# A hybrid attention and FFN layer on one core: operands of down in the tiles of gate/up, last norms on VectorE, additions on POOL, scores two units ahead, and inputs interleaved

## The chip, the cores and the metric

The kernel runs on 1 core of one Trainium2 chip. The metric is the device time of one execution in microseconds (us). A core has five engines with instruction queues of their own: PE (TensorE, matmuls), DVE (VectorE), ACT (ScalarE), POOL (GpSimd), and SP (SyncE), which here issues all the transfers. Each queue runs in order. SBUF is the working memory, PSUM takes the results of matmuls.

## The reference, cut to what matters

One decoder layer over 1024 tokens of width 1024, in float32. One input projection feeds two groups of heads: four differential-attention heads (each the difference of two softmaxes) and eight heads with three branches (compressed, selected, window). One output projection follows, then a residual, a layer norm, a SwiGLU network of width 2816, a residual and a second layer norm.

```python
h = x @ w_in[l]
...
blk = kv[:, idx] + pe[None, None, :, None, :]          # compress_kv
return jax.nn.gelu(blk @ w1) @ w2
...
a = p[:, :, 0] - lam * p[:, :, 1]                      # diff_attention, per block of queries
...
mix = jnp.concatenate([o_diff, o_nsa], axis=-1) @ w_out[l]
x = layer_norm(DEEPNORM_ALPHA * x + mix, ln1_g[l], ln1_b[l])
ffn = (jax.nn.silu(x @ w_gate[l]) * (x @ w_up[l])) @ w_down[l]
x = layer_norm(DEEPNORM_ALPHA * x + ffn, ln2_g[l], ln2_b[l])
```

## The kernel before

Every float32 operand of a large matmul is split in a high part (the rounded form that TensorE takes, written by ScalarE) and a low part (the rest, by VectorE or POOL: `split`, L81 and L83), and a product is three matmuls, high by high, high by low and low by high (`mm3`, L116 to L118). The function is written in stages. A scheduler of the framework orders the instructions of each engine by their place in the source, moved by explicit priorities, and by a simulated time at which each is ready. Tiles come from pools: a tag with `bufs=n` has n places, and a new tile waits until the old one in its place is no longer used.

*Start.* Three blocks of w_in (`w3`) and x transposed (`load_x`, half of the tokens at a time) are loaded and split; three products run beside each other. The first block of weights is loaded in two pieces ahead of the first piece of x. The low part of the first block is made on VectorE, of the others on POOL. The results are copied out of PSUM (L243 to L247), and `compress` adds the position terms to them (L197, eight instructions), multiplies (L207) and applies gelu. Between these, the weights of values and gates (`w_vg`, three pieces) are split and projected for eight blocks of rows.

*Attention.* Each phase has units of a front (scores, the fused scale, distance and minimum L308, exponentials) and a back (transposes L330, the split of the transposed tile, products with the values). A unit takes one or two of six t tiles. `LOOK` is 1: a unit's back is written after the front of the next unit. Fillers (projections for later phases, loads of w_out) are spread between the units. The last phases are diff(2) and diff(3), in two halves each.

*Output and x.* `out_start` loads a row block of the mixed heads and splits it, `out_half` multiplies by w_out, `norm1` normalises. For the FFN x is cut in four quadrants, and sums of them (T1 to T4, by `x_sums`) feed a Strassen-like scheme with seven products in place of eight. X 11, 21, T3 and T2 have eight tiles of 8 KB per partition in the pool pb, with four half tiles; 22, T1 and T4 lie in big and w tiles.

*Gate and up.* 11 pairs of blocks; each step multiplies by all seven operands, and VectorE and POOL combine the results. The operands of down for each pair are written to DRAM: `hidden_operands` (a_d, L980 to L988) and `down_weights` (t_d, L968 to L974). The order of the products in a step is 11, 21, T3, T1, 22, T2, T4.

*Down.* The pool pb is closed and the pool pc with nine op tiles opened in its place. Seven products of 11 steps each follow, in the order 1, 2, 6, 5, 3, 7 and 4. A step (`down_operand`) loads a piece of a_d and a piece of t_d (L1042, L1043), splits them, and runs 12 matmuls. The first six steps use op tiles, later ones alternate between big and op. Rows 0 to 3 are normalised after product 3, rows 4 to 7 at the end, where the last product runs row by row; of these, two rows use ScalarE, POOL and VectorE in turn (L617 to L619), and two `vector_only` (L609, L611). The reciprocal root (L129, L130) is always on POOL.

Of the kernel before, what the change touches and what calls it, by code (L numbers as in the profile page):

```python
# [17 lines left out]
P = 128  # L18
# [6 lines left out]
NCMP = 63  # L25
WIN_BLOCKS = 5
AHEAD = 1.25
LOOK = 1

BACK_LATER = 60  # L30
FILL_LATER = 2000
# [8 lines left out]
def layer_kernel(ctx: ExitStack, tc: tile.TileContext, xT, x, w_t, w_vg, w_dv, lam_in, subln,  # L40
# [53 lines left out]
    def load_split_here(src, hi, lo, l_eng="dve", order=(0,)):  # L94

        n = 1024 // len(order)
        for k in order:
            raw = lo[:, k * n:(k + 1) * n].bitcast(F32)
            nc.sync.dma_start(raw, src[:, k * n:(k + 1) * n])
            split(raw, hi[:, k * n:(k + 1) * n], lo[:, k * n:(k + 1) * n], l_eng)  # L100
        return hi, lo

    def w_tiles():
        lo = w_tile()
        return w_tile(), lo
# [38 lines left out]
    with ExitStack() as ctx_a:  # L144
# [44 lines left out]
        def compress(c, A):  # L189
            blk = [slot(6 * c + 2 + n, F32) for n in range(2)]  # L190
            for jh in range(2):
                bv = blk[jh].rearrange("p (j g n) -> p j g n", j=8, g=2)
                nc.gpsimd.memset(bv[:, :, :, 63:64], 0.0)
                for g in range(2):
                    src = A[g].rearrange("p (n j s) -> p j n s", j=8, s=2)[:, :, :, 0]
                    lo = src[:, :, jh:jh + 63]
                    nc.vector.tensor_add(bv[:, :, g, 0:63], lo,  # L197
                                         pes[:, c, jh * 8:(jh + 1) * 8].unsqueeze(2).to_broadcast([P, 8, 63]))
            w1s = []
            for jh in range(2):  # L200
                w = slot(6 * c + 4 + jh, F32)
                nc.sync.dma_start(w, w1[:, c, jh, :])
                w1s.append(w)
            hp = ps_m()
            for jh in range(2):
                for j in range(8):
                    nc.tensor.matmul(hp[:, :P], lhsT=w1s[jh][:, j * P:(j + 1) * P],  # L207
                                     rhs=blk[jh][:, j * P:(j + 1) * P],
                                     start=(jh == 0 and j == 0), stop=(jh == 1 and j == 7))
            xg = small([P, P], "tmp", 3)  # L210
            sg = small([P, P], "ms", 2)
            nc.vector.tensor_copy(xg, hp[:, :P])
            nc.vector.tensor_mul(sg, xg, xg)
            nc.vector.tensor_scalar(sg, sg, 0.044715, 1.0, op0=ALU.mult, op1=ALU.add)
            nc.vector.tensor_mul(sg, sg, xg)
            nc.scalar.activation(sg, sg, AF.Tanh, scale=float(math.sqrt(2.0 / math.pi)))
            nc.vector.scalar_tensor_tensor(sg, sg, 1.0, xg, op0=ALU.add, op1=ALU.mult)
            nc.vector.tensor_scalar(sg, sg, 0.5, None, op0=ALU.mult)
            return sg
# [343 lines left out]
        def out_start(i):  # L563

            acc[i] = slot((8, 9, 10, 11, 4, 2, 3, 5)[i], F32)
            nc.sync.dma_start(acc[i], x[i * P:(i + 1) * P, :])
            mix_rows[i] = load_split_here(mix_d[i].rearrange("p k t -> p (k t)"), *w_tiles(), order=(1, 0))

        def out_half(i, nh, ps):
            m = mix_rows[i]  # L570
# [68 lines left out]
            return pa.tile([P, 1024], dt, tag="t", name="t", bufs=6)  # L639


        w3 = [load_split(w_t[0], *w_tiles(), pieces=2)]
        load_x(0, 0, 2)
        w3.append(load_split(w_t[1], *w_tiles(), land=slot(8, F32), l_eng="pool", pieces=2))
        w3.append(load_split(w_t[2], t_tile(), t_tile(), land=slot(9, F32), l_eng="pool", pieces=2))
        for hf in range(2):
# [65 lines left out]
        def qf(p, hf):  # L712
            return q_fill(4 + p, hf, qn[p])
# [19 lines left out]
        def held_fill():  # L733
# [8 lines left out]


        phases = [
            (nsa(0), [qf(0, 1), kf(0), qf(1, 0), kf(1)], 1, 0),
            (nsa(1), [qf(1, 1), dvf(0, range(8)), wo_copy(0), qf(2, 0)], 1, 0),
            (nsa(2), [qf(2, 1), kdf(0, 0), wo_copy(1), qf(3, 0), kdf(0, 1)], 1, 0),
            (nsa(3), [qf(3, 1), kdf(1, 0), qdf(0, 0), kdf(1, 1)], 1, 0),
            (diff(0), [qdf(0, 1), dvf(1, range(4)), qdf(1, 0)], 1, 0),
            (diff(1), [qdf(1, 1), dvf(1, range(4, 8)), kdf(2, 0), kdf(2, 1), qdf(2, 0)], 1, 0),  # L750
            (diff(2, 0, 4), [kdf(3, 0), kdf(3, 1), qdf(3, 0)], 0, 0),
            (diff(3, 0, 4), [qdf(2, 1)], 0, 0),
            (diff(2, 4), [wo_fill(0), qdf(3, 1), wo_fill(1), held_fill(), out_fill(0, False), out_fill(1, False)], 0, 0),
            (diff(3, 4), [ln_fill((0, 1)), out_fill(2, True), out_fill(3, True)], 0, 0),
        ]
        pending = []

# [7 lines left out]
                tc.cur_priority -= BACK_LATER  # L765
            finish_held()

        for make, fillers, due, after in phases:
            units = make()
            total = sum(u[2] for u in units[:-1])  # L770
            due_cost = sum(f[1] for f in fillers[:due])
            rate = sum(f[1] for f in fillers) / total if after == 0 else sum(f[1] for f in fillers[due:]) / (total - after)
            queue = [f[0] for f in fillers]
            run = {"gen": None, "spent": 0.0, "closed": 0}

            def pump(at, first=0):
                if after:
                    goal = due_cost * min(1.0, at / after) + max(0.0, at - after) * rate
                else:
                    goal = at * rate * AHEAD  # L780
                while run["spent"] < goal or run["closed"] < first:
                    if run["gen"] is None:
                        if not queue:
                            return
                        run["gen"] = queue.pop(0)()
                    tc.cur_priority += FILL_LATER
                    c = next(run["gen"], None)
                    tc.cur_priority -= FILL_LATER
                    if c is None:
                        run["gen"] = None  # L790
                        run["closed"] += 1
                    else:
                        run["spent"] += c

            at = 0.0
            for n, (front, back, cost) in enumerate(units):
                if n == len(units) // 2:
                    pump(0, due)
                front()
                pending.append((back, at, cost))  # L800
                if len(pending) > LOOK:
                    finish_unit(pump)
                at += cost
            pump(1e9, 99)

            pending = [(p[0], 0.0, 0.0) for p in pending]
# [9 lines left out]

    x_work = ExitStack()
    pb = x_work.enter_context(tc.tile_pool(name="pb", bufs=1, reuse_waits="tile"))  # L820
    LO, HI = slice(0, 512), slice(512, 1024)

    def x_tile(name):
# [26 lines left out]
    def x_sums(i):  # L850

        b11, b21 = acc[i - 4][:, LO], acc[i - 4][:, HI]
        b12, b22 = acc[i][:, LO], acc[i][:, HI]
        t3, t2 = half_tile(2 * (i % 2)), half_tile(2 * (i % 2) + 1)
        nc.vector.tensor_sub(b11, b12, b11)
        nc.vector.tensor_sub(t3, b22, b12)
        x_put("T3", i, t3)
        nc.vector.tensor_sub(t2, b22, b11)
        x_put("T2", i, t2)
        nc.vector.tensor_sub(b21, b21, t2)  # L860

    def out_half_now(i, nh, ps):
        for _ in out_half(i, nh, ps):
# [159 lines left out]

    x_work.close()
    pc = ctx.enter_context(tc.tile_pool(name="pc", bufs=1, reuse_waits="tile"))

    A_AT = {1: 0, 2: 1, 4: 2, 5: 3, 6: 4, 7: 5, 3: 6}
    B_AT = {1: 0, 2: 1, 3: 2, 5: 3, 6: 4, 7: 5, 4: 6}  # L1030
    n_step = [0]

    def place():

        n_step[0] += 1
        return "big" if n_step[0] > 6 and n_step[0] % 2 else "op"

    def down_operand(n, p, where):

        op = big_tile() if where == "big" else pc.tile([P, 2, 1024], F32R, tag="op", name="op", bufs=9)  # L1040
        raw = op[:, 1, :].bitcast(F32)
        nc.sync.dma_start(raw[:, LO], a_d[p, A_AT[n]])  # L1042
        nc.sync.dma_start(raw[:, HI], t_d[p, B_AT[n]])  # L1043
        split(raw, op[:, 0, :], op[:, 1, :])
        return op
# [22 lines left out]
        dst = acc[i][:, part]  # L1068
        nc.vector.scalar_tensor_tensor(dst, dst, ALPHA, src, op0=ALU.mult, op1=ALU.add)

    us, ws = halves(3, 9), halves(10, 11)
    bs = banks()
    down(1, bs)
    for j in range(4):
        nc.scalar.copy(us[j], bs[j])
        residual(j, slot((2, 4, 5, 8)[j], F32))
    down(2, bs, True)
    for j in range(4):
        add_to(j, LO, bs[j])
# [16 lines left out]
    bs = banks()  # L1096
    ops = []
    for p in range(NP):
        op = down_operand(7, p, "op")
        for j in range(4):  # L1100
            mm_down(bs[j], op, j, p == 0, p == NP - 1, False)
        ops.append(down_operand(4, p, "big" if p < 8 else "op"))
    st = []
    for j in range(4):
        add_to(j + 4, HI, bs[j])
# [5 lines left out]
    for j in range(4):  # L1111
        for p, op in enumerate(ops):
            mm_down(bs[j], op, j, p == 0, p == NP - 1, False)
        dst = acc[j + 4][:, LO]
        nc.vector.tensor_add(dst, dst, bs[j])
        layer_norm(acc[j + 4], out[(j + 4) * P:(j + 5) * P, :], vector_only=j >= 2, st=st[j])


# [61 lines left out]
```

## Time and profile before

| | |
|---|---|
| three runs | 1369.91, 1371.19, 1373.59 us; median 1371.19 |
| the profiled execution | 1370.36 us, its span 1368.6 us |
| busy in the span | PE 1313.8, DVE 954.8, ACT 653.6, POOL 447.6 us |
| mean granted clock of TensorE | 0.981 of 2.4 GHz |
| moved by transfers | 184.17 MB, 135 GB/s in the mean |

The time of an execution is 1.8 us longer than the span of its instructions. Busy times are means over stages that have different limits. A granted clock of 1 is 2.4 GHz, of 0.5 is 1.2 GHz; a mean between them is a share of each. PE's busy time counts matmuls that overlap, and a busy PE isn't always a PE at its full rate.

### The profile page before, as it was taken

The numbers are of one execution on the slowest core, as the hardware profiler recorded it, in microseconds if no ns is written. First come the engines' busy times: TensorE is split into PE (matmuls) and PEld (weight loads), VectorE is DVE, ScalarE is ACT, GpSimd is POOL, SyncE is SP. The second block draws the span as 40 slices with busy tenths as digits, with TensorE's granted clock in tenths as the row PEclk, the third lists the DMA queues.
The fourth block names the chain that finished last, engine by engine and source line by source line (L and its number), as shares of the span: only waits on it lengthen the run. The fifth ranks groups of instructions, "written<-read, shape, count | busy, mean of one in ns | idle before, by whom it ended". The sixth has DMA issues, their size and how long they took to land.

```text
span 1368.6 us, 20323 instructions
## 1 busy us (share of the span) xinstructions
PE 1313.8 (96%) x7002; PEld 1127.3 (82%) x7002; DVE 954.8 (70%) x1952; ACT 653.6 (48%) x1331; POOL 447.6 (33%) x450
## 2 busy tenths in 40 slices
PE   8899999999999999799999999999999995999996
PEld 6898998888899987688877888888888884888885
DVE  5646767878796757884797768777677646655586
ACT  5335676777785656653344333333333324543330
POOL 5114354453543636633312323233223220000063
PEclk9999999999999999899999999999999997999998
DMA  9402012120303226323313556555555479766641
GB/s 364 114 18 53 23 45 60 30 63 7 77 19 81 76 56 202 118 82 131 101 70 100 207 177 200 185 174 179 171 176 180 147 251 390 264 196 193 191 147 62
DMA packets 86983, 184.17 MB, mean 135 GB/s; under 512 B 10592, under 2 KB 19168, under 8 KB 86752
## 3 DMA queue, kind: packets, MB, share of 16 engines
q1 hardware_dynamic: 86880, 182.87, 41.1%
q8 instruction: 55, 0.90, 0.3%
q14 instruction: 48, 0.39, 0.1%
HBM read 117.23 MB, written 57.15 MB: 127 GB/s over the span
## 4 chain that ended last, share of the span: by engine, by line
PE 82%; DVE 7%; DMA 3%; POOL 2%; issue 1%; ACT 1%; SPq 0%; POOLq 0%; DVEq 0%; ACTq 0%
PE psM L116 9%; PE psM L117 9%; PE psM L118 9%; PE psT L330 5%; PE psT L117 5%; PE psS L116 5%; PE psT L118 5%; PE psS L118 5%; PE psT L116 5%; PE psS L117 5%; PE psS L304 3%; PE psS L305 3%; PE psO L409 2%; PE psO L407 2%; PE psO L117 2%; PE psO L116 2%
## 5 line engine op out<-in xcount | busy, mean ns | idle before, releaser
L321 ACT ACTIVATE t<-t,m 128x128 f32<-128x128 f32 (+7 forms) x192 | 144.3, 752 | 55.2 <-DVE m L308 48.7
L392 POOL TENSOR_SCALAR t<-t,r,gates 128x640 f32<-128x640 f32 (+7 forms) x128 | 100.7, 789 | 160.5 <-DVE r L391 108.5
L83 DVE TENSOR_TENSOR pt<-psT,pt 128x512 fp32r<-128x512 f32 (+2 forms) x200 | 117.3, 598 | 21.5 <-ACT pt L81 20.0
L116 PE MATMUL psM<-big,w 128*128 128x512 f32 x304 | 122.6, 403 | 0.6 <-DVE q L177 0.6
L117 PE MATMUL psM<-big,w 128*128 128x512 f32 x304 | 121.1, 398 | 0.0
L118 PE MATMUL psM<-big,w 128*128 128x512 f32 x304 | 121.1, 399 | 0.0
L81 ACT CAST pt<-psT 128x512 fp32r<-128x512 f32 (+2 forms) x200 | 99.7, 519 | 37.1 <-PE psT L330 19.5
L304 PE MATMUL psS<-slot,q 128*128 128x320 f32 (+5 forms) x288 | 108.2, 377 | 5.2 <-DVE m L308 4.7
L330 PE MATMUL psT<-ident,t 128*128 128x128 f32 x672 | 110.0, 276 | 2.7 <-ACT tmp L487 2.3
L948 POOL TENSOR_TENSOR half<-half,half 128x512 f32<-128x512 f32 x22 | 32.5, 1476 | 212.7 <-ACT half L947 212.7
L305 PE MATMUL psS<-slot,q 128*128 128x320 f32 (+5 forms) x288 | 97.4, 339 | 0.0
L330 PEld LDWEIGHTS psT<-ident,t 128*128 128x128 f32 x672 | 81.2, 142 | 9.4 <-ACT tmp L487 3.0
L308 DVE CUSTOM_DVE_ANT_0 t<-psS,dsel 128x512 f32<-128x512 f32 (+5 forms) x128 | 68.1, 534 | 29.7 <-PE psS L305 27.1
L83 DVE TENSOR_TENSOR op<-op 128x1024 fp32r<-128x1024 f32 x44 | 57.7, 1311 | 41.7 <-ACT op L81 40.9
L83 DVE TENSOR_TENSOR big<-slot,big 128x1024 fp32r<-128x1024 f32 (+1 forms) x53 | 65.0, 1234 | 24.9 <-ACT big L81 24.9
L81 ACT CAST big<-slot 128x1024 fp32r<-128x1024 f32 (+1 forms) x53 | 54.0, 1034 | 52.7 <-DVE slot L940 47.4
L81 ACT CAST big<-big 128x1024 fp32r<-128x1024 f32 (+1 forms) x49 | 44.6, 914 | 65.6 <-DMA big<-t_d 57.4
L81 ACT CAST op<-op 128x1024 fp32r<-128x1024 f32 x44 | 46.3, 1052 | 59.3 <-DMA op<-t_d 57.5
L409 PE MATMUL psO<-pt,slot 128*128 128x256 f32 x264 | 72.6, 296 | 0.6 <-DVE pt L83 0.5
L407 PE MATMUL psO<-pt,slot 128*128 128x256 f32 x264 | 71.6, 287 | 0.0
L83 DVE TENSOR_TENSOR big<-big 128x1024 fp32r<-128x1024 f32 x33 | 42.2, 1278 | 36.6 <-ACT big L81 36.3
L116 PEld LDWEIGHTS psM<-big,w 128*128 128x128 f32 x304 | 57.9, 190 | 11.9 <-DVE q L177 1.0
(365 smaller groups left out, 3973.5 us busy)
## 6 DMA issues: line engine op xcount, KB each, us to landing
a_d<-slot SPq DMA_DIRECT2D x77, 256.0 KB, 3.0
t_d<-slot SPq DMA_DIRECT2D x77, 256.0 KB, 2.2
q<-q SPq DMA_DIRECT2D x48, 256.0 KB, 3.0
slot<-in_w_up_dram SPq DMA_DIRECT2D x22, 512.0 KB, 4.1
slot<-in_w_down_dram SPq DMA_DIRECT2D x22, 512.0 KB, 4.2
op<-a_d SPq DMA_DIRECT2D x44, 256.0 KB, 3.0
op<-t_d SPq DMA_DIRECT2D x44, 256.0 KB, 3.7
big<-a_d SPq DMA_DIRECT2D x33, 256.0 KB, 2.7
```

What stands on the lines that cost most here:

```text
L81: nc.scalar.copy(hi, src)
L83: eng.tensor_sub(lo, src, hi.bitcast(F32))
L116: nc.tensor.matmul(acc, lhsT=ah, rhs=bh, start=first, stop=False, skip_group_check=more)
L117: nc.tensor.matmul(acc, lhsT=ah, rhs=bl, start=False, stop=False, skip_group_check=more)
L118: nc.tensor.matmul(acc, lhsT=al, rhs=bh, start=False, stop=last, skip_group_check=more)
L304: nc.tensor.matmul(ps[:, :w], lhsT=q[0], rhs=k[:, ks], start=True, stop=False)
L305: nc.tensor.matmul(ps[:, :w], lhsT=q[1], rhs=k[:, ks], start=False, stop=True)
L321: nc.scalar.activation(t[:, :width], t[:, :width], AF.Exp, bias=m, scale=-1.0, accum_out=r)
L330: nc.tensor.transpose(tp[:rows, n * P:(n + 1) * P], s, ident)
L392: nc.gpsimd.tensor_scalar(ts[a][:, :width], ts[a][:, :width], r[:, a:a + 1], gates[:, i, gc:gc + 1], op0=ALU.mult, op1=ALU.mult)
L407: nc.tensor.matmul(po[:, :256], lhsT=v, rhs=pt[:, 0, n * 256:(n + 1) * 256], start=False, stop=False)
L409: nc.tensor.matmul(po[:, :256], lhsT=v, rhs=pt[:, 1, n * 256:(n + 1) * 256], start=False, stop=last)
```

## The change

Six things change. The start loads x and w in turn, with eight small matmuls on the identity ahead. Compress' additions go from VectorE to POOL. In the last four phases the back of a unit is written after the fronts of the next two. The low parts of mix for rows 4 to 7, and one subtraction of `x_sums`, go from VectorE to POOL. Down's operands use the tiles of X (six, then four big, two, four big, and so on), pb stays open and pc goes; three slots of residuals and of partial results are others. The last four rows all use `vector_only`.

```diff
-                    nc.vector.tensor_add(bv[:, :, g, 0:63], lo,
+                    nc.gpsimd.tensor_add(bv[:, :, g, 0:63], lo,
...
-            mix_rows[i] = load_split_here(mix_d[i].rearrange("p k t -> p (k t)"), *w_tiles(), order=(1, 0))
+            mix_rows[i] = load_split_here(mix_d[i].rearrange("p k t -> p (k t)"), *w_tiles(),
+                                           "dve" if i < 4 else "pool", order=(1, 0))
...
-        w3 = [load_split(w_t[0], *w_tiles(), pieces=2)]
-        load_x(0, 0, 2)
+        warm = ps_o()
+        for _ in range(8):
+            nc.tensor.matmul(warm[:, :P], lhsT=ident, rhs=ident, start=True, stop=True)
+        xs[0, 0], raw_x = big_tiles(), slot(0, F32)
+        w3, raw_w = [w_tiles()], w_tile(F32)
+        for k in range(2):
+            cs = slice(k * 512, (k + 1) * 512)
+            nc.sync.dma_start(raw_x[:, cs], xT[0, 0][:, cs])
+            nc.sync.dma_start(raw_w[:, cs], w_t[0][:, cs])
+            for raw, t in ((raw_x, xs[0, 0]), (raw_w, w3[0])):
+                split(raw[:, cs], t[0][:, cs], t[1][:, cs])
...
-            (diff(2, 0, 4), [kdf(3, 0), kdf(3, 1), qdf(3, 0)], 0, 0),
+            (diff(2, 0, 4), [kdf(3, 0), kdf(3, 1), qdf(3, 0)], 0, 0, 2),
...
-        for make, fillers, due, after in phases:
+        for make, fillers, due, after, look in phases:
...
-                if len(pending) > LOOK:
+                while len(pending) > look:
                     finish_unit(pump)
...
-    x_work = ExitStack()
-    pb = x_work.enter_context(tc.tile_pool(name="pb", bufs=1, reuse_waits="tile"))
+    pb = ctx.enter_context(tc.tile_pool(name="pb", bufs=1, reuse_waits="tile"))
...
-        nc.vector.tensor_sub(b21, b21, t2)
+        nc.gpsimd.tensor_sub(b21, b21, t2)
...
-    x_work.close()
-    pc = ctx.enter_context(tc.tile_pool(name="pc", bufs=1, reuse_waits="tile"))
...
+    X_TAGS = ["x11h", "x11l", "x21h", "x21l", "xT3h", "xT3l", "xT2h", "xT2l"]
+
+    PLACES = X_TAGS[:6] + ["big"] * 4 + X_TAGS[6:] + ["big"] * 4
...
-        return "big" if n_step[0] > 6 and n_step[0] % 2 else "op"
+        return PLACES[(n_step[0] - 1) % len(PLACES)]
...
-        op = big_tile() if where == "big" else pc.tile([P, 2, 1024], F32R, tag="op", name="op", bufs=9)
+        op = big_tile() if where == "big" else pb.tile([P, 2, 1024], F32R, tag=where, name="op")
...
-    us, ws = halves(3, 9), halves(10, 11)
+    us, ws = halves(5, 9), halves(10, 11)
...
-        residual(j, slot((2, 4, 5, 8)[j], F32))
+        residual(j, slot((2, 4, 3, 6)[j], F32))
...
-        op = down_operand(7, p, "op")
+        op = down_operand(7, p, X_TAGS[p % 8])
...
-        ops.append(down_operand(4, p, "big" if p < 8 else "op"))
+        ops.append(down_operand(4, p, "big" if p < 8 else X_TAGS[p - 5]))
...
-        layer_norm(acc[j + 4], out[(j + 4) * P:(j + 5) * P, :], vector_only=j >= 2, st=st[j])
+        layer_norm(acc[j + 4], out[(j + 4) * P:(j + 5) * P, :], vector_only=True, st=st[j])
```

## Rows read from the trace of the kernel before

**Rows 1.** The page: TensorE's busy time, share of the span, instructions; its weight loads.

```profile
PE 1313.8 (96%) x7002; PEld 1127.3 (82%) x7002; DVE 954.8 (70%) x1952; ACT 653.6 (48%) x1331; POOL 447.6 (33%) x450
```

**Rows 2.** Waits of TensorE, whole span: waiting for, total us, times, longest us.

```profile
PE psS L116 <- ACT op L81: 16.5, 1, 16.5
...
PE psT L117 <- DVE t L83: 3.4, 1, 3.4
PE psT L839 <- DVE mv L604: 3.4, 1, 3.4
```

**Rows 3.** Windows: us, then busy us (instructions) by engine, clock, DMA share, GB/s.

```profile
6.80:13.20 6.40, 6.38 (x14) 4.75 (x15) 2.36 (x3) 4.91 (x7) 5.88 (x21) 1.00 1.03 394
...
55.20:61.00 5.80, 5.79 (x25) 5.79 (x26) 5.67 (x7) 1.21 (x2) 2.13 (x2) 0.51 0.74 179
543.00:590.00 47.00, 37.86 (x190) 31.74 (x188) 36.88 (x112) 30.46 (x86) 25.13 (x26) 0.82 0.45 133
...
1146.20:1149.80 3.60, 3.60 (x9) 2.82 (x10) 1.60 (x2) 1.20 (x2) 0.00 (x0) 0.51 1.05 404
...
1160.00:1170.00 10.00, 10.00 (x46) 8.27 (x45) 7.35 (x8) 5.38 (x6) 0.00 (x0) 1.00 1.05 393
...
1357.60:1368.60 11.00, 0.01 (x1) 0.00 (x0) 6.95 (x11) 0.00 (x0) 3.22 (x4) 0.67 0.37 143
```

**Rows 4.** Timeline of the first 22 us: start us, us, engine, operation, idle before.

```profile
2.02 0.29 POOL masks.py:199 TENSOR_SCALAR_AFFINE_SELECT ident<-ident 128x128 f32<-128x128 f32 x1
...
6.82 0.79 PE L116 MATMUL psS<-big,w 128*128 128x512 f32 x1 [6.82 <-ACT big L81]
...
11.76 3.54 POOL L83 TENSOR_TENSOR t<-slot,t 128x512 fp32r<-128x512 f32 x2
```

**Rows 5.** Compress' additions (ns min/median/max, first to last), and VectorE's timeline.

```profile
L197 DVE TENSOR_TENSOR slot<-t,pes x8: 1033/1053/1983, 47.5 to 61.2; 128x504 f32<-128x504 f32 x8
...
53.94 1.22 DVE L83 TENSOR_TENSOR t<-w,t 128x840 fp32r<-128x840 f32 x1
```

**Rows 6.** Operations on POOL (busy us, mean ns), and one line on VectorE.

```profile
L83 POOL TENSOR_TENSOR w<-w 128x512 fp32r<-128x512 f32 x36 | 47.2, 1327 | 47.4 <-ACT w L81 44.1 <-ACT t L321 2.4 <-DMA w<-in_w_t_dram 0.8
...
L363 POOL TENSOR_TENSOR pc<-pc,cst 128x512 f32<-128x512 f32 x8 | 8.4, 1045 | 6.9 <-DVE cst L362 5.8 <-DVE r L391 1.2
...
L860 DVE TENSOR_TENSOR slot<-slot,half x4: 677/680/692, 680.4 to 715.4; 128x512 f32<-128x512 f32 x4
```

**Rows 7.** Timelines of VectorE and POOL near 728.

```profile
728.20 1.78 DVE L939 TENSOR_TENSOR slot<-slot,slot 128x512 f32<-128x512 f32 x1
...
728.14 1.29 POOL L948 TENSOR_TENSOR half<-half,half 128x512 f32<-128x512 f32 x1 [20.32 <-ACT half L947]
```

**Rows 8.** Waits from 505 to 600.

```profile
PE psS L304 <- DVE m L308: 2.8, 6, 1.1
```

**Rows 9.** Timelines of TensorE, POOL and SP around the first product of down.

```profile
1112.99 0.39 PE L118 MATMUL psO<-x11h,big 128*128 128x512 f32 x1
...
1134.53 1.64 POOL L1018 TENSOR_TENSOR slot<-half,slot 128x512 f32<-128x512 f32 x1 [3.16 <-DVE half L955]
...
1138.54 0.32 SPq L1042 DMA_DIRECT2D op<-a_d  x1
...
1142.54 0.32 SPq L988 DMA_DIRECT2D a_d<-slot  x1
...
1154.33 0.33 SPq L965 DMA_DIRECT2D slot<-in_w_down_dram  x1
...
1170.84 0.42 SPq L1043 DMA_DIRECT2D big<-t_d  x1
```

**Rows 10.** Timelines of POOL and VectorE in the last 20 us.

```profile
1353.59 2.40 POOL L618 TENSOR_TENSOR w<-w,slot 128x1024 f32<-128x1024 f32 x1 [1.60 <-ACT w L617]
...
1360.58 0.68 DVE L1115 TENSOR_TENSOR w<-w,psM 128x512 f32<-128x512 f32 x1
```

**Rows 11.** The page: DMA issues by line, KB each, median us to landing.

```profile
slot<-in_w_down_dram SPq DMA_DIRECT2D x22, 512.0 KB, 4.2
```

More of the change, by code (lines that the diff above doesn't have):

```diff
@@ L27 @@
 AHEAD = 1.25
-LOOK = 1
 BACK_LATER = 60
@@ L744, in layer_kernel @@
         phases = [
[L745 to L750, printed above, removed]
-            (diff(2, 0, 4), [kdf(3, 0), kdf(3, 1), qdf(3, 0)], 0, 0),
-            (diff(3, 0, 4), [qdf(2, 1)], 0, 0),
-            (diff(2, 4), [wo_fill(0), qdf(3, 1), wo_fill(1), held_fill(), out_fill(0, False), out_fill(1, False)], 0, 0),
-            (diff(3, 4), [ln_fill((0, 1)), out_fill(2, True), out_fill(3, True)], 0, 0),
+            (nsa(0), [qf(0, 1), kf(0), qf(1, 0), kf(1)], 1, 0, 1),
+            (nsa(1), [qf(1, 1), dvf(0, range(8)), wo_copy(0), qf(2, 0)], 1, 0, 1),
+            (nsa(2), [qf(2, 1), kdf(0, 0), wo_copy(1), qf(3, 0), kdf(0, 1)], 1, 0, 1),
+            (nsa(3), [qf(3, 1), kdf(1, 0), qdf(0, 0), kdf(1, 1)], 1, 0, 1),
+            (diff(0), [qdf(0, 1), dvf(1, range(4)), qdf(1, 0)], 1, 0, 1),
+            (diff(1), [qdf(1, 1), dvf(1, range(4, 8)), kdf(2, 0), kdf(2, 1), qdf(2, 0)], 1, 0, 1),
+            (diff(2, 0, 4), [kdf(3, 0), kdf(3, 1), qdf(3, 0)], 0, 0, 2),
+            (diff(3, 0, 4), [qdf(2, 1)], 0, 0, 2),
+            (diff(2, 4), [wo_fill(0), qdf(3, 1), wo_fill(1), held_fill(), out_fill(0, False), out_fill(1, False)], 0, 0, 2),
+            (diff(3, 4), [ln_fill((0, 1)), out_fill(2, True), out_fill(3, True)], 0, 0, 2),
         ]
```

## The prediction

> **What bounds the kernel now.** I read the page first. TensorE is busy for 96% of the span [rows 1], so its work is the floor and only its idle time and its slow-clock time can be won here: no part of the diff removes a matmul of the computation (it adds eight small ones at the start). The share alone says nothing of where the rest lies, so the next view is TensorE's waits [rows 2]: one wait of 16.5 us, where down begins, and many of a few us. The windows then give, for each such stretch, the idle time and the granted clock [rows 3]; a wait is usually followed by a stretch at the lower level (1.2 of 2.4 GHz), whose cost has to be added. The timelines of the other engines show what came late at each place [rows 4, 5, 9, 10]. The reader should see five separate losses, each with its own cause, and a TensorE that is full between them: what is won at one place is passed on to the end.
>
> **The change part by part.** The sum is made against the profiled execution: 1370.36 us, that is a span of 1368.6 and 1.8 around it. It lies 0.8 below the median of the three runs.
>
> *Start (warm-up matmuls, x and w interleaved).* TensorE starts at 6.82, when the first split of x is done; that load is issued after both pieces of the weights. It then issues 14 matmuls in 6.4 us [rows 3, 4], against 46 in 10 us later on [rows 3]: at the full level these 14 take 3.0, so 3.4 us are lost to the clock. The identity is ready at 2.02 + 0.29 = 2.31, so the warm-ups can run from there and keep TensorE active some 4 us sooner. But a faster TensorE meets its data: the low half of the third weight tile is on POOL from 11.76 to 15.3 [rows 4], and warm-ups at the lower level may themselves last until the first real operands are there. Bounds 0 and 3.4 plus 0.8 for the earlier first matmul = 4.2. I take the middle, 2.
>
> *Compress' eight additions to POOL (L197).* On VectorE each takes 1.05 us in the median, from 47.5 on [rows 5]. The split of the second piece of w_vg starts only at 53.94, behind four of them (4.2 us or more); TensorE waits 3.4 us for it [rows 2] and then runs 5.8 us at a clock of 0.51, which costs 5.8 x 0.49 = 2.8. With the four gone from ahead of it the split is not late: 6.2 us are to be won. On POOL such an addition is not in the trace. The nearest rows are a broadcast subtraction of 128x512 at 1.05 us and a plain one at 1.33 [rows 6], so eight take 8 to 11 us there. What they hold back are the compress matmuls; the cover is the projection of w_vg, which TensorE can run in the meantime. If that cover fails, POOL's 11 us against VectorE's own 8 x 1.05 = 8.4 bring the compress matmuls some 3 us later, and the win is 3. Bounds 0 and 6.2; I take 5.
>
> *Splits of mix for rows 4 to 7, and one subtraction of x_sums, to POOL.* Eight splits and four subtractions leave VectorE, 0.68 us each when nothing disturbs them, and become POOL's at 1.33 (both in [rows 6]). Where x is summed, TensorE waits 3.4 us behind a dense VectorE (L604 in [rows 2]), so a relief would count there. But the rows show the price. At 728.20 a VectorE subtraction with both inputs in SBUF takes 1.78 us: it ends 0.55 us after the POOL addition that began at 728.14 and took 1.29 [rows 7]. So an operation moved to POOL can hold VectorE for longer than the operation itself took. Taken at 1.1 us (1.78 less 0.68) for the two subtractions ahead of that wait, against 1.36 us removed, nothing is left. I take 0, with -3 and +4 as ends: at worst four holds of 1.1 with 1.4 taken back, at best the wait of 3.4 and a little clock.
>
> The Trainium skill has this as a rule. "SBUF — State Buffer", in its section on the ports, says that VectorE operations with two SBUF inputs and POOL operations that read SBUF take one shared port pair as an exclusive lock. "GPSIMD Engine Reference", Engine selection, advises VectorE for elementwise additions, POOL being about twice as slow with two inputs. The trace agrees (1.33 against 0.68, and the hold to 1.78). By that rule alone, all twenty moved operations are a loss: the terms of compress and of x_sums would be 0 and below instead of 5 and 0, and the sum 8 us smaller (an estimate from these pages' rule with this trace's times).
>
> *Scores two units ahead in diff(2) and diff(3).* Sixteen units are affected. From 543 to 590 TensorE is idle for 47.0 - 37.9 = 9.1 us, and the clock is 0.82, some 17 us of the 47 at the lower level [rows 3], of which half is lost where TensorE is busy: at most 7 us. But the waits of score matmuls for the fused scale-and-minimum L308 to free their bank sum to only 2.8 us between 505 and 600 [rows 8]; the other waits there are for splits, loads of w_out and the sums of outputs, which come no sooner because more scores are ahead. I take 3. Ends: +16, and -5 if the six t tiles, now all taken by three units of two, make VectorE wait.
>
> *Operands of down in X's tiles.* Before, the nine op tiles lie in a pool that takes the place of the one that holds X and the half tiles. The last use of a half tile is the POOL multiplication from 1134.53 to 1136.2, and the first op load goes out at 1138.54 [rows 9], in the middle of transfers for later steps. After, the first six operands go into the tiles of X 11, 21 and T3. The last matmul with x11h is issued at 1112.99 [rows 9], 17 us before TensorE runs dry at 1146.2 - 16.5 = 1129.7. The loads and splits of the first steps then lie beside the last up product, and the 16.5 us go, with 3.6 x 0.49 = 1.8 us at a clock of 0.51 behind them [rows 3]: 18.3. What is late next: the eleventh step of down(1) needs the last pair of down's weights. Before, the last store of the hidden operands goes out at 1142.54, the load of w_down behind it at 1154.33, and the load of that step's operand at 1170.84 [rows 9], 28 us in all. SP is in order, and these stood behind a row of op loads. The stores can now come at about 1137 (after 1129.7 one sum, one POOL multiplication of 1.64 and four sums of 0.68 take 5 us, and SP some 2), as this chain is no longer held by splits that wait for loads. TensorE reaches the step at 1129.7 + 10 x 12 / 4.6 = 1156. Three transfers of at most 4.2 us [rows 11] and a split on ScalarE and VectorE (about two operations of 0.68 on each, 2.5 us) put the operand there at 1152 when the queue is free, and 28 us and the splits at 1167 when it is as full as before. So this gives 18.3 at best and 18.3 - 11 = 7 at worst. I take 15, nearer to the free queue, since the early loads no longer crowd into the same 20 us.
>
> *Last norms on VectorE.* The last matmul ends at 1357.6, but its bank is added only at 1360.58 [rows 3, 10]: VectorE is still at the row before, held by the pass of an earlier row on POOL (2.40 us from 1353.59) and the rsqrt queued behind it. With all four rows on VectorE, a row costs about 4.3 us (sum, statistics and four passes at 0.68 each, the aggregate 0.2) against 11 x 3 / 4.6 = 7.2 us of TensorE for each, so it keeps up: 3.0 us. Ends 1.5 and 3.
>
> **Sum.** 2 + 5 + 0 + 3 + 15 + 3 = 28; 1370.4 - 28 = 1342.4. I forecast 1343 against the median's slightly higher base.
>
> **The rivals.**
> 1. *The wait moves to the eleventh step of down(1).* For it: the 28 us above, and transfers that stay as many as they were. Against: the loads now start 17 us sooner, and down(6) has other banks and can be taken first. 15 becomes 7, with a little lost behind it: 1351 to 1354.
> 2. *The moves to POOL cost what they take off.* For it: the hold in [rows 7]. Against: the copies out of PSUM that stand in VectorE's queue beside them read no SBUF. Win at compress 0, x_sums -3: 1343 + 8 = 1351.
> 3. *More than forecast:* two units ahead fill most of 543 to 590 (12 instead of 3) and the whole 18.3 go at down: 1343 - 12 = 1331. For it: a stall there lowers the clock, which lengthens the next; against: [rows 8].
> 4. *Slower.* The t tiles are full at three units, so that L308 of a new unit waits in VectorE's queue until the unit before last is transposed, and the splits behind it wait too. Price per unit p, sixteen units, in place of the win of 3: at 3.4 us a unit (the length of the two VectorE waits in [rows 2]) 54 - 25 = 29 us slower, 1399. It decides from 25 / 16 = 1.6 us a unit. Against: the back of the unit that frees the tiles is issued before the scores that need them.
> 5. *No change at down:* the X tiles are reused but their loads still queue late: the 15 are lost, 1358.
>
> **How the numbers follow.** Forecast 0.42, rival 1 0.17, rival 2 0.12, rival 3 0.16, rival 4 0.04, rival 5 0.05; 0.04 for losses that cancel the win in another way. The likeliest gives 1343, by itself 1337 to 1349. For 8 in 10 the range reaches from 1330, just below rival 3, to 1356, above rivals 1 and 2. Faster by over 0.3% (4 us, about what a measurement of this kernel can tell from no change) 0.92, within it 0.03, slower 0.05.
>
> **What would show it.** In the trace after: no TensorE wait over 5 us where the first product of down begins, op loads into x11h from about 1113 less what was won before; L197 on POOL and no 3.4 us wait for L83 at w_vg; the last bank added within 0.3 us of the last matmul; TensorE at the full level before its fifteenth real matmul. The prediction is wrong if a new wait of over 8 us appears at the eleventh step of down, or if VectorE's idle time grows in the sixteen units.

## The result and the profile after

The changed kernel takes 1356.04 us (median of 4 runs, 1355.6 to 1357.84) beside 1370.55 for the kernel before on the same chip: a ratio of 0.9893, with a 95% interval of 0.9875 to 0.9911. That is 14.5 us won where 28 were forecast, and the time stands at the very end of the range that was given (1330 to 1356). The profiled execution has a span of 1354.2 us beside 1368.6, 14.4 less. Lines of the code up to about 565 have moved up by one, those from the sums of x on down by nine. Of the kernels below, one run of norms_before took 1866.1 us at a mean granted clock of 0.652 and is left out of every number.

Three points of the trace divide the 14.4 us. TensorE's last up product ends at 1128.3 instead of 1129.7: everything ahead of down brought 1.4 (forecast 10). Its last matmul ends at 1346.3 instead of 1357.6, so down brought 9.9 more (forecast 15). From there to the end are 7.9 instead of 11.0, 3.1 more (forecast 3).

Every trace holds the same 7002 matmuls of the computation, so two kernels can be compared by when TensorE begins the same one of them in the count. By that the changed kernel is ahead of the kernel before by 0.3 us at the latter's 45 us, 5.6 at 500, 6.2 at 640, 6.6 at 690, 1.4 at 730 and 1.4 at the boundary to down. So what the first 690 us win is almost all lost again where x is summed.

The page's line for TensorE, and its longest waits over the whole span (total us, times, longest us):

```profile
PE 1312.3 (97%) x7018; PEld 1121.8 (83%) x7018; DVE 946.6 (70%) x1936; ACT 649.9 (48%) x1329; POOL 475.2 (35%) x468
```

```profile
PE psS L303 <- DVE m L307: 7.3, 16, 1.6
PE psT L848 <- DVE half L865: 5.3, 1, 5.3
PE psO L115 <- ACT big L80: 4.2, 1, 4.2
PE psM L115 <- ACT w L80: 2.8, 1, 2.8
...
PE psS L115 <- ACT op L80: 1.6, 1, 1.6
```

The 16.5 us wait of [rows 2] is gone, and so is the 3.4 us wait for w_vg. In their place stand 5.3 us at the sums of x (3.4 before, L839 in [rows 2]) and 4.2 and 1.6 within down. The 2.8 is in the score stage, at 583, for the high part of a w tile. The windows (same columns as in [rows 3]) show what each of these cost with the clock behind it:

```profile
55.20:61.00 5.80, 5.80 (x54) 5.80 (x53) 1.22 (x3) 0.61 (x2) 5.72 (x6) 1.00 0.37 83
543.00:590.00 47.00, 36.71 (x193) 29.25 (x194) 37.09 (x117) 30.99 (x86) 25.06 (x25) 0.93 0.37 106
700.00:710.00 10.00, 7.13 (x23) 5.50 (x24) 5.17 (x9) 2.88 (x5) 2.90 (x2) 0.53 0.34 134
1115.00:1155.00 40.00, 40.00 (x178) 33.14 (x177) 27.50 (x25) 18.55 (x19) 9.88 (x5) 1.00 1.05 400
1155.00:1160.00 5.00, 0.80 (x4) 0.34 (x3) 3.94 (x4) 3.53 (x4) 0.00 (x0) 0.99 1.04 393
1160.00:1170.00 10.00, 10.00 (x39) 8.11 (x38) 8.15 (x9) 4.09 (x5) 0.00 (x0) 0.83 0.82 286
1170.00:1175.00 5.00, 3.39 (x15) 2.36 (x13) 3.19 (x4) 2.67 (x3) 0.00 (x0) 1.00 1.05 386
```

At 55.2 the clock is at its upper level (0.51 in [rows 3]). Where x is summed it falls to 0.53 for 10 us, which costs 7.13 x 0.47 = 3.4 us on top of the wait. TensorE runs through the boundary to down without a gap, and then loses 4.2 us of idle time, 10 x 0.17 = 1.7 us of clock and 1.6 us of idle time, 7.5 in all.

VectorE and POOL where x is summed (start us, us, then the operation):

```profile
688.40 2.31 DVE L82 TENSOR_TENSOR big<-slot,big 128x1024 fp32r<-128x1024 f32 x2
...
695.32 2.58 DVE L609 SCALAR_TENSOR_TENSOR slot<-slot,mv,slot 128x512 f32<-128x512 f32 x2
697.82 1.21 DVE L619 TENSOR_TENSOR slot<-slot,slot 128x1024 f32<-128x1024 f32 x1
698.95 1.40 DVE L611 SCALAR_TENSOR_TENSOR slot<-slot,mv,slot 128x512 f32<-128x512 f32 x2
700.27 0.68 DVE L864 TENSOR_TENSOR slot<-slot,slot 128x512 f32<-128x512 f32 x1
700.88 0.68 DVE L865 TENSOR_TENSOR half<-slot 128x512 f32<-128x512 f32 x1
...
688.57 1.05 POOL L128 TENSOR_SCALAR mv<-mv 128x1 f32<-128x1 f32 x1 [7.13 <-DVE mv L604]
689.71 1.41 POOL L129 TENSOR_TENSOR mv<-mv,mhalf 128x1 f32<-128x1 f32 x1
693.19 3.49 POOL L618 TENSOR_TENSOR slot<-slot,slot 128x1024 f32<-128x1024 f32 x1 [2.08 <-ACT slot L617]
```

L609 and L611 are the norm of row block 7; L619 ends that of row block 6, and L864 and L865 are x_sums(6), for which TensorE waits. In the kernel before, VectorE ran L619 and x_sums(6) first and the norm of row block 7 after them. Two lines of the kernel before (L855 is x_sums(6), L609 the norm of row block 7):

```profile
704.80 0.67 DVE L855 TENSOR_TENSOR slot<-slot,slot 128x512 f32<-128x512 f32 x1
...
706.67 1.40 DVE L609 SCALAR_TENSOR_TENSOR slot<-slot,mv,slot 128x512 f32<-128x512 f32 x2
```

Now the order of the planner (the framework's scheduler) has row block 7 ahead, and the two hold each other up: L609's pair takes 2.58 us beside POOL's L618 and L618 3.49, against 1.40 just above and 2.40 in [rows 10].

SP's queue and TensorE in down, with the last of the sums (L995) whose stores are L997:

```profile
1128.10 0.39 PE L115 MATMUL psS<-op 128*128 128x512 f32 x1
...
1138.55 0.68 DVE L995 TENSOR_TENSOR slot<-slot,slot 128x512 f32<-128x512 f32 x1
...
1147.44 0.40 SPq L997 DMA_DIRECT2D a_d<-slot  x1
...
1157.80 0.33 SPq L974 DMA_DIRECT2D slot<-in_w_down_dram  x1
...
1159.66 0.60 PE L115 MATMUL psO<-big 128*128 128x512 f32 x1 [4.20 <-ACT big L80]
...
1174.03 0.73 PE L115 MATMUL psS<-op 128*128 128x512 f32 x2 [1.61 <-ACT op L80]
```

TensorE began down(1) at 1128.10 and its last product in the banks psS and psM began at 1155.07, which is room for ten steps. The eleventh needs the last pair of w_down, whose first tile was only asked for at 1157.80. So steps of down(6), whose banks are psO and psT, come next in TensorE's queue, and it had to wait for their operand as well; psS went on at 1174.03. By the count of matmuls the lead over the kernel before falls from 19.9 us at its 1155 to 11.3 at its 1200, which is 8.6.

### The profile page after: what moved, and what is told of

Same layout as the page of the kernel before. It is cut to its first block, busy times and chain, and to the rows that moved or that the text cites. A ratio compares the mean times of both kernels' runs of the same rounds, so it can differ in the third digit from the quotient of the medians.

```text
span 1354.2 us, 20369 instructions
## 1 busy us (share of the span) xinstructions
PE 1312.3 (97%) x7018; PEld 1121.8 (83%) x7018; DVE 946.6 (70%) x1936; ACT 649.9 (48%) x1329; POOL 475.2 (35%) x468
## 4 chain that ended last, share of the span: by engine, by line
PE 85%; DMA 6%; DVE 5%; ACT 2%; issue 1%; SPq 0%; POOLq 0%; DVEq 0%; POOL 0%; ACTq 0%
PE psM L115 10%; PE psM L116 10%; PE psM L117 9%; PE psT L329 5%; PE psS L115 5%; PE psT L115 5%; PE psS L117 5%; PE psT L117 5%; PE psS L116 5%; PE psT L116 5%; PE psS L303 3%; PE psS L304 3%; PE psO L408 2%; PE psO L406 2%; DMA big<-t_d 2%; PE psO L115 2%
## 5 line engine op out<-in xcount | busy, mean ns | idle before, releaser
L82 DVE TENSOR_TENSOR pt<-psT,pt 128x512 fp32r<-128x512 f32 (+2 forms) x200 | 117.8, 599 | 20.0 <-ACT pt L80 18.3
L303 PE MATMUL psS<-slot,q 128*128 128x320 f32 (+5 forms) x288 | 106.5, 371 | 8.4 <-DVE m L307 7.3
L304 PE MATMUL psS<-slot,q 128*128 128x320 f32 (+5 forms) x288 | 95.6, 333 | 0.0
L307 DVE CUSTOM_DVE_ANT_0 t<-psS,dsel 128x512 f32<-128x512 f32 (+5 forms) x128 | 68.3, 535 | 27.5 <-PE psS L304 24.3
L82 DVE TENSOR_TENSOR op<-op 128x1024 fp32r<-128x1024 f32 x44 | 62.7, 1432 | 35.1 <-ACT op L80 34.8
L303 PEld LDWEIGHTS psS<-slot,q 128*128 128x128 f32 x288 | 54.7, 190 | 18.5 <-DVE m L307 14.2
```

What stands on the lines that cost most here:

```text
L82: eng.tensor_sub(lo, src, hi.bitcast(F32))
L303: nc.tensor.matmul(ps[:, :w], lhsT=q[0], rhs=k[:, ks], start=True, stop=False)
L304: nc.tensor.matmul(ps[:, :w], lhsT=q[1], rhs=k[:, ks], start=False, stop=True)
```

## The experiments

Each kernel is the changed kernel with the edit shown. Medians are beside 1356.04. The number behind a median is its ratio to the kernel before, which was run beside each, with its 95% interval. The difference in us is that of two such ratios (0.9893 for the changed kernel), times 1370. Each ratio's interval is about 0.002 either way, so that a difference below some 4 us isn't resolved by the times alone.

**The last w_down tile in another slot.** Theory: the tile waits for slot 11, which the hidden operands' q1 holds until its stores. Rival: the transfers are full (DMA share 1.05 from 1115 to 1155), so a sooner load only shifts the queue.

```
-        f1, f2 = slot(11, F32), slot(9, F32)
+        f1, f2 = slot(8 if p == NF // 2 - 1 else 11, F32), slot(9, F32)
```

> The changed kernel, with the first w_down tile of the last pair (f1 of down_weights(10)) in slot 8 in place of slot 11, which q1 of the last hidden_operands holds until its stores. In the changed kernel's trace f1 was issued at 1157.80, PE ran out of steps of down(1) at 1155.07 and lost 4.2 us of idle time, 1.65 us of clock and 1.6 us of idle time before 1175, 7.5 us in all. Theory (the slot): f1 is issued before 1120, the eleventh step of down(1) follows the tenth on PE, and the run takes 1348 to 1351 us beside 1356 of the changed kernel. Rival (the transfers: DMA share 1.03 to 1.06 from 1115 to 1160): operands come no sooner, another step waits about as long, and the run takes 1354 to 1357.

Measured: 1347.8 us, 0.9835 (0.9813 to 0.9856), 7.9 us less. Its SP queue (the second of the two loads, at 1099.5, is that of the last pair) and windows:

```profile
1098.20 1.65 SPq L974 DMA_DIRECT2D slot<-in_w_down_dram  x2
```

```profile
1155.00:1160.00 5.00, 5.00 (x23) 4.14 (x23) 1.26 (x2) 2.94 (x6) 0.00 (x0) 1.00 1.04 393
1160.00:1170.00 10.00, 10.00 (x45) 8.26 (x45) 7.64 (x7) 6.82 (x8) 0.00 (x0) 1.00 1.05 388
1170.00:1175.00 5.00, 5.00 (x24) 4.13 (x22) 4.53 (x5) 4.12 (x4) 0.00 (x0) 1.00 0.91 313
```

The load goes out 58 us sooner and all 7.5 us are back, with the DMA share as high as before up to 1170. The slot held it, not the transfers.

**The sums of x: which part made the wait.** Three kernels. The first leaves the moved operations on POOL and takes the norm of row block 6 off ACT and POOL; the second and third each undo one of the two moves.

```
row6_vector
-    norm1(6)
+    norm1(6, vector_only=True)
mix_vector
-    ... *w_tiles(), "dve" if i < 4 else "pool", order=(1, 0))
+    ... *w_tiles(), order=(1, 0))
b21_vector
-        nc.gpsimd.tensor_sub(b21, b21, t2)
+        nc.vector.tensor_sub(b21, b21, t2)
```

> The changed kernel, with the norm of row block 6 whole on VectorE as that of row block 7 is, so that x_sums(6) no longer waits for POOL's multiplication (3.49 us at 693.19) nor stands behind the norm of row block 7 on VectorE (L609 and L611 from 695.32 to 700.27). All additions moved to POOL stay there. Theory (order): the 5.28 us stall of PE before the transposes of x_sums(6) falls under 1.5 us and the run takes 1350 to 1353 beside 1356. Rival (the moved additions themselves hold VectorE at the shared port): the stall stays over 3 us and the run takes 1355 to 1357.

> The changed kernel, with the splits of the mix rows 4 to 7 back on VectorE (b21 stays on POOL). Theory (the splits queue on POOL ahead of the norm of row 6, which puts VectorE's norm of row 7 ahead of x_sums(6)): the stall before the transposes of x_sums(6) falls from 5.28 to 1 to 3.4 us, and the run takes 1352 to 1354. Rival (the lead of the scores alone brought the rows together): the stall stays over 4.5 us and the time within 1 us of 1356.

> The changed kernel, with the subtraction into b21 of x_sums back on VectorE (the splits of the mix rows stay on POOL). In the changed kernel POOL takes 1.29 to 1.45 us for each of the four and VectorE is idle beside most of them. Theory (order): nothing changes for PE, 1355 to 1357. Rival (the moved addition is what VectorE is held by): 1351 to 1354.

Measured: row6_vector 1348.88 us, 0.9847 (0.9829 to 0.9864), 6.3 less; mix_vector 1348.66, 0.9845 (0.9824 to 0.9865), 6.6 less; b21_vector 1357.76, 0.9917 (0.9897 to 0.9936), 3.3 more by the ratios and not resolved. TensorE's wait at x_sums(6) in the three, in that order, with VectorE's first line of x_sums(6) (L864, in mix_vector L863) and its first of the norm of row block 7 (L609, L608):

```profile
699.24 1.91 PE L848 MATMUL psT<-ident,half 128*128 128x128 f32 x8 [2.48 <-DVE mv L604]
...
697.82 0.67 DVE L864 TENSOR_TENSOR slot<-slot,slot 128x512 f32<-128x512 f32 x1
699.69 1.40 DVE L609 SCALAR_TENSOR_TENSOR slot<-slot,mv,slot 128x512 f32<-128x512 f32 x2
```

```profile
697.09 1.59 PE L847 MATMUL psT<-ident,half 128*128 128x128 f32 x8 [2.31 <-DVE mv L603]
...
695.67 0.67 DVE L863 TENSOR_TENSOR slot<-slot,slot 128x512 f32<-128x512 f32 x1
697.54 1.40 DVE L608 SCALAR_TENSOR_TENSOR slot<-slot,mv,slot 128x512 f32<-128x512 f32 x2
```

```profile
700.74 1.09 PE L848 MATMUL psT<-ident,half 128*128 128x128 f32 x4 [6.10 <-DVE half L865]
...
695.51 1.41 DVE L609 SCALAR_TENSOR_TENSOR slot<-slot,mv,slot 128x512 f32<-128x512 f32 x2
699.30 0.68 DVE L864 TENSOR_TENSOR slot<-slot,slot 128x512 f32<-128x512 f32 x1
```

In the first two, VectorE has x_sums(6) ahead of the norm of row block 7 again; in b21_vector it doesn't, and the wait stays. So the wait follows the order on VectorE. By the count of matmuls, TensorE loses 5.2 us against the kernel before between the latter's 690 and 730 in the changed kernel and 5.9 in b21_vector; it gains 0.4 in row6_vector and loses 0.3 in mix_vector. Both of the first two gained more than the wait alone, as the clock behind it stayed up as well. For mix_vector the windows from 500 to 645 also show some 3 us less of idle and slow time. That need not be the splits: start_before and compress_vector (below), whose edits lie elsewhere, win 4.5 and 4.3 us on the kernel before between 500 and 640, mix_vector 4.0 and the changed kernel 0.6. The wait that is left in row6_vector, 2.48 us, is longer than the 1.5 expected, and the time is better than expected by 1 us; mix_vector's is better than expected by 3, and b21_vector's 0.8 above its range.

**Both repairs together.**

> The changed kernel with both repairs: the last pair's w_down tile in slot 8 and the norm of row block 6 whole on VectorE. By itself the first took 8 us and the second 6 us off the changed kernel, at places 450 us apart. Theory (two separate waits): the gains add, 1340 to 1344 us. Rival (a row block that comes sooner meets the same transfers at the boundary to down): 1346 to 1349.

Measured: 1341.53 us, 0.9793 (0.9768 to 0.9818), 13.7 less than the changed kernel and about 28 less than the kernel before. The gains add (7.9 + 6.3 = 14.2). It is the fastest kernel of the study.

**Scores one unit ahead, and the same with both repairs.**

```
-            (diff(2, 0, 4), [kdf(3, 0), kdf(3, 1), qdf(3, 0)], 0, 0, 2),
+            (diff(2, 0, 4), [kdf(3, 0), kdf(3, 1), qdf(3, 0)], 0, 0, 1),
...
```

> The changed kernel with the scores of the four last stages one unit ahead, as before the change. By the prediction's term alone (3 us) it takes 1358 to 1360. By the order theory it loses 2 to 4 us in the sixteen units and wins 4 to 7 us where the rows 6 and 7 meet, since VectorE then has x_sums(6) ahead of the norm of row 7 as in the kernel before: 1351 to 1354. A time under 1350 would say that the lead of two has no gain in its own stage.

> Both repairs (slot 8, norm of row 6 on VectorE), but the scores of the four last stages one unit ahead. The order of the rows is then the same with either lead, so this prices the lead of two alone. By the prediction's term (3 us; 2.5 us read from the trace of the changed kernel) it takes 1343.5 to 1346 beside 1341.5 for the kernel with both repairs. Rival (the lead has no gain of its own): 1340 to 1343.

Measured: 1353.3 us, 0.9875 (0.9853 to 0.9896), 2.5 less without the lead and not resolved; with both repairs 1342.52, 0.9787 (0.9762 to 0.9812), beside 1341.53 and 0.9793. Undoing the lead also undid the bad order: TensorE's wait at x_sums(6) is 2.49 us there. By the count of matmuls it is 6.2 us ahead of the changed kernel at the boundary to down, and only 1.9 at the end: in down it waits 3.7 and 3.2 us where the changed kernel waits 4.2 and 1.6, and loses more to the clock. So the time of scores_one alone hides most of what the order costs. With the order settled by the repairs, the windows of the stage give, with one unit ahead and with two:

```profile
500.00:645.00 145.00, 133.55 (x724) 112.87 (x724) 102.19 (x270) 80.31 (x210) 70.26 (x69) 0.96 0.41 128
```

```profile
500.00:645.00 145.00, 133.13 (x730) 111.20 (x729) 101.93 (x272) 80.79 (x212) 71.86 (x69) 0.99 0.43 133
```

The idle time is the same (11.5 and 11.9 us); the clock loses less with two, and six more matmuls fit. But the medians differ by 1.0 us one way and the ratios by 0.8 the other, with overlapping intervals; 1342.52 lies in the range of the rival, no gain. Between 500 and 640 by the count of matmuls, the eleven kernels with a lead of two win 0.6 to 4.5 us on the kernel before (2.4 in the mean), the two with a lead of one 0.2 and 0.8. So a gain of some 2 us is likely in this stage, and no time here settles it.

**The mix splits, where the order is settled.** Both repairs, with the mix splits on VectorE.

> Both repairs, with the splits of the mix rows 4 to 7 on VectorE. This prices the moved splits where the norm of row 6 no longer passes through POOL. By the prediction (0 us, bounds 3 us lost to 4 us gained) it takes 1340 to 1343. By the theory that the splits were dear only by the order they made, the same. Rival (they hold VectorE wherever they stand): 1336 to 1339.

Measured: 1342.78 us, 0.9793 (0.9767 to 0.9818), the same ratio as with them on POOL. The moved splits by themselves cost nothing and win nothing that the times resolve.

**The other parts, each undone by itself.**

```
compress_vector
-                    nc.gpsimd.tensor_add(bv[:, :, g, 0:63], lo,
+                    nc.vector.tensor_add(bv[:, :, g, 0:63], lo,
down_before
-        op = big_tile() if where == "big" else pb.tile([P, 2, 1024], F32R, tag=where, name="op")
+        op = big_tile() if where == "big" else pc.tile([P, 2, 1024], F32R, tag="op", name="op", bufs=9)
...
start_before
-        warm = ps_o()
...
+        w3 = [load_split(w_t[0], *w_tiles(), pieces=2)]
+        load_x(0, 0, 2)
norms_before
-        layer_norm(..., vector_only=True, st=st[j])
+        layer_norm(..., vector_only=j >= 2, st=st[j])
```

> The changed kernel with the eight additions of compress back on VectorE (0.68 us each and more there, 1.44 on POOL). By the prediction's term (5 us: PE waits for VectorE's splits of w_vg again) it takes 1360 to 1362. Rival (the interleaved start already brings w_vg in time): 1355 to 1358.

> The changed kernel with the operands of down in a pool of their own, opened when gate/up's closes, and us and the residuals in their slots of before. By the losses between 1100 and 1185 (18.3 us before, 7.7 after) it takes 10 to 11 us more than the changed kernel, 1365 to 1368, with a wait of PE of 15 to 17 us for op at the first step of down(1). By the prediction's term (15 us) it would be 1370 to 1372.

> The changed kernel with the start of before: no products to warm up, the first weights asked for as a whole tile ahead of the first inputs. By the prediction's term (2 us) 1357.5 to 1359.5. Rival (the start is gone again before the first scores): 1355 to 1357.

> The changed kernel with the last norms of j = 0 and 1 on ACT, POOL and VectorE again. By the prediction's term (3 us; 3.1 us between the last products of PE and the end in the trace) 1358 to 1360. Rival (the last row block ends the kernel anyway): 1355 to 1357.

Measured: compress_vector 1360.94 us, 0.9936 (0.9915 to 0.9956), 5.9 more; down_before 1364.97, 0.9962 (0.9947 to 0.9978), 9.5 more; start_before 1354.41, 0.9877 (0.9856 to 0.9898), 2.2 less and not resolved; norms_before 1359.06, 0.992 (0.9895 to 0.9945), 3.7 more with intervals that overlap. TensorE in compress_vector and in down_before:

```profile
53.89 0.40 PE L116 MATMUL psT<-t,big 128*128 128x280 f32 x1 [2.71 <-DVE t L82]
```

```profile
1143.91 1.22 PE L115 MATMUL psS<-op 128*128 128x512 f32 x2 [15.49 <-ACT op L80]
```

Each of these waits is back where its part is undone. By the count of matmuls compress_vector is 4.4 us behind the changed kernel at 500. For the start, the windows of the first 30 us, in the changed kernel and in start_before:

```profile
0.00:30.00 30.00, 25.60 (x104) 19.77 (x105) 16.03 (x19) 15.72 (x22) 17.41 (x48) 1.00 0.93 346
```

```profile
0.00:30.00 30.00, 23.23 (x88) 18.23 (x89) 16.50 (x19) 15.59 (x22) 18.15 (x48) 1.00 0.97 364
```

The warm-ups are 16 of the 104 records, so both have 88 of the computation after 30 us. The changed kernel is ahead at first (14 of them by 12 us, against 12), but it waits for splits (0.23, 0.89 and 0.73 us, up to 12.57), where start_before doesn't wait at all from 6.76 to 30. At 45 us the two are within 0.2 us. That start_before takes 2.2 us less isn't from the start: it wins 4.5 us between 500 and 640, as said above.

## Why the prediction was about half right

The measured 1356.04 lies at the end of the range, which reached that far for the sake of rivals 1 and 2; it is 7 us above the forecast's own 1337 to 1349. By the trace the winning terms came to 0.3 + 5.3 + 1.0 ahead of the sums of x, 9.9 in down and 3.1 at the end, with 5.2 lost at the sums.

*Start: 2 forecast, 0 found.* The step named the right limit ("a faster TensorE meets its data") and gave it half the weight that it has. The warm-ups did what they were for: the third to the thirteenth matmul begin 0.43 us apart in start_before, and in the changed kernel 0.23 from the tenth on wherever operands are there. The waits for splits took that back. That the slow start is "lost to the clock" is not shown: the granted clock in that row of [rows 3] reads 1.00, and only the spacing says otherwise.

*Compress: 5 forecast, 4 to 6 found* (4.4 by the trace, 5.9 by the times). The mechanism holds: in the changed kernel VectorE is done with w_vg at 54.6, no wait is left, and POOL's longer additions are hidden:

```profile
L196 POOL TENSOR_TENSOR slot<-t,pes x8: 1282/1322/2113, 46.8 to 57.0; 128x504 f32<-128x504 f32 x8
```

The eight run from 46.8 to 58.3, 11.5 us where 8 to 11 were forecast. The rule of the Trainium skill that I had weighed ("GPSIMD Engine Reference", Engine selection) would have made this term 0; compress_vector decides against it here: POOL is slower by the addition (1.32 us against 1.05 in the median), but VectorE had a split to do that TensorE waited for.

*Mix splits and x_sums: 0 forecast, 5 to 6.5 lost* (5.2 by the trace against the kernel before, 6.3 and 6.6 by the times of the kernels with the order back). This is the first step that failed, and its bound of -3 as well. I priced the moved operations by how long they hold VectorE. What they changed was when row block 6 and row block 7 become ready, and with it the order in which the planner puts two norms and a sum on VectorE. Shown: the wait goes when the order goes back, whether by the splits, by the scores or by the norm of row 6, and the splits cost nothing where the order is safe. Not shown is by which single time the planner's choice tips.

*Scores: 3 forecast, some 2 found in the stage and not settled,* and the lead too is needed for the bad order. The same 6 us must not be counted for both parts: either one undone brings them back at the sums of x. The mechanism is only in part the one forecast: TensorE's waits for the fused scale-and-minimum (L308 before, L307 after) do not shrink but grow, from 2.8 us to 4.9 between 500 and 645, and what is won there is clock (0.82 before and 0.93 after in 543 to 590).

*Down: 15 forecast, 9.5 to 9.9 found.* The wait of 16.5 went as forecast. The step that failed is "the stores can now come at about 1137". The sums were done at 1139.2, two us after the stores were to go out, and the stores of L997 went out from 1142.81 to 1147.44, among op loads in SP's queue and no sooner than the 1142.54 of [rows 9]. The last of them landed at 1153.1, and only then was the slot of w_down free; its load went out at 1157.80, behind other loads in the queue, and took 6.6 us to land ("at most 4.2" was a median in [rows 11]). I had counted the transfers of a chain and left out that the chain's first link is a buffer. This is rival 1, at the place it names and with 7.5 us of the 11 it allowed; a wait of over 8 us, which I had put as the mark of a wrong prediction, didn't come. With the slot free, down gives 9.5 + 7.9 = 17.4, the 18.3 of the best case but for 0.9.

*Last norms: 3 forecast, 3.1 found in the trace* (3.7 by the times, not resolved). The last matmul and VectorE's last addition from its bank, after and in norms_before:

```profile
1345.88 0.39 PE L117 MATMUL psM<-op 128*128 128x512 f32 x1
...
1346.31 0.69 DVE L1124 TENSOR_TENSOR w<-w,psM 128x512 f32<-128x512 f32 x1 [1.34 <-PE psM L117]
```

```profile
1344.66 0.39 PE L117 MATMUL psM<-op 128*128 128x512 f32 x1
...
1347.51 0.68 DVE L1124 TENSOR_TENSOR w<-w,psM 128x512 f32<-128x512 f32 x1
```

VectorE now waits for TensorE instead of being late by 2.5 us.

*The rivals.* Rival 2 had a loss where x is summed, half as large and by another cause, and its loss at compress didn't come. Rival 4's full tiles don't show: VectorE is as busy in 543 to 590 as before (37.1 against 36.9 us). Over 500 to 645 its idle time did grow, which the prediction had put as a mark of being wrong, from 41.2 to 43.9 us; but it is 43.3 with the lead of one (scores_one), so the lead isn't what made it. The forecast of 1343 was missed by 13 us through two waits, and the kernel with both of them repaired takes 1341.5. That this comes so close is in part luck: down then gives 2 us more than forecast, the start 2 less.

## What to carry to other kernels

When an operation is moved between engines under a list scheduler, read the order on the relieved engine anew: what costs is less the operation than who now comes first, and a row that takes two engine hops can be overtaken by one that takes none. When a load is made early, follow it back to the buffer it lands in and to that buffer's last reader, before counting transfers. And two losses 450 us apart on a full TensorE added here when both were repaired; but what is won ahead of a wait that isn't repaired can be lost in it again, as scores_one shows (6.2 us ahead at the boundary to down, 1.9 at the end).

## What the runs showed of the hardware

The hold between VectorE and POOL works in both directions. In [rows 7] VectorE's subtraction took 1.78 us instead of 0.68; here POOL is held, and its smallest operations suffer most in proportion. Beside VectorE's two 128x1024 splits at 688.40 (above), POOL's 128x1 operations L128 and L129 took 1.05 and 1.41 us; in mix_vector, where no such split ran beside them, 0.19 and 0.55:

```profile
682.76 0.19 POOL L128 TENSOR_SCALAR mv<-mv 128x1 f32<-128x1 f32 x1 [2.05 <-DVE mv L603]
683.03 0.55 POOL L129 TENSOR_TENSOR mv<-mv,mhalf 128x1 f32<-128x1 f32 x1
```

The Trainium skill ("SBUF — State Buffer", SBUF: two separate sides) describes an exclusive lock on a port pair that the two engines share, held for a whole instruction. These rows agree with it, and here the held operations lie on the chain of a norm that TensorE waits for.

Beside transfers at a share of 1.05 and 400 GB/s TensorE was busy for all of 40 us at a clock of 1.00 (1115 to 1155 in the changed kernel), and in wdown_slot8 from 1155 to 1175 as well.
